# Attention of two layers: scores and products with values as plain fp32 on halves of the array

## The chip, the cores and the metric

The kernel runs on one core of a Trainium2 chip. The metric is the device time of one execution in microseconds, as the median of several runs. The program is one launch that holds four layers of a network.

## The reference

Four layers (kinds A, B, C, A) work on two token streams: 128 context tokens and 512 latent tokens. Layers 0 and 3 are of kind A: attention with 16 query heads of 64 channels over 4 key heads, so 4 query heads share one key head. Latent queries see 256 cached tokens and a window of 128 tokens to either side; context queries see the 128 context tokens. Each head has a sink, a constant score that takes part in the softmax and has no value.

```python
def attend_block(q, k, v, valid, sink):
    scale = q.shape[-1] ** -0.5
    s = jnp.einsum('bqkgd,bskd->bkgqs', q, k, preferred_element_type=jnp.float32) * scale
    if valid is not None:
        s = jnp.where(valid, s, -jnp.inf)
    if sink is not None:
        sk = jnp.broadcast_to(sink.astype(jnp.float32)[None, :, :, None, None], s.shape[:-1] + (1,))
        probs = jax.nn.softmax(jnp.concatenate([s, sk], axis=-1), axis=-1)[..., :-1]
...
    return jnp.einsum('bkgqs,bskd->bqkgd', probs.astype(v.dtype), v)
```

Ahead of it stand a dense product to queries, keys and values, a norm of each head and a rotary embedding; behind it a dense product back to 1024 channels. Layer 2 (kind C) has heads of 128 channels and no window; layer 1 is a recurrence. Each layer ends with a channel mixer, a convolution between two large dense products, which take most of the time of the program.

## The kernel before

All work is laid out by hand in the class `Kernel`; a scheduler of the framework sets the final order on each engine. TensorE (PE) multiplies, ScalarE (ACT) and VectorE (DVE) evacuate and compute, GpSimd (POOL) takes some elementwise work, and SP issues the transfers.

**Two-part operands.** An fp32 number is kept as two parts of the type fp32r: a rounded one (h) and the rest (l). A dense product is then three fp32r products (`mm3`, lines 294 to 296 of the kernel's listing). Splitting costs a copy on ACT and a subtraction on DVE or POOL (`split`, lines 299 and 303 do the copy and the subtraction wherever `split` and `copy` are called).

**Attention of kind A** is cut into 16 units: for each of the 4 key heads (`kv`) the query tiles 0, 1, 2, and 3 together with 4 (tile 4 is the context). A `Unit` has these steps:

- `qprep` (lines 83 to 91): POOL makes the two parts of the queries of 4 heads, side by side as 128 columns; four transposes on PE (line 88); ACT copies the result (`QT`), whose 128 rows are the 64 of h and the 64 of l.
- `kprep` (lines 951 to 972), once per key head, in steps between other work: the keys in two parts, each part twice side by side, so that the transposed `KT` has both parts on 128 rows; 14 transposes (line 967). The values become `V2`: h and l side by side as 128 columns.
- `score(g)` (lines 112, 113): for each run of keys two fp32r products, queries times keys h and queries times keys l, each with all 128 rows. Together they are the complete product of the parts. The scores of a head have 512 columns for tile 0, 256 + 384 for tiles 1 and 2, and 512 and 128 for the unit of tiles 3 and 4. DVE adds the mask and takes the maximum (line 123), ACT does the exponential (line 126).
- `turn(j)` (line 178): the probabilities of one tile of 128 keys are transposed for the 4 heads, 4 fp32 transposes; then they are split to `PTh` (ACT) and `PTl` (DVE), 512 columns each.
- `pv(j)` (lines 203, 204): two products with `V2`, with 512 columns. The output has the products with values h on partitions 0 to 63 and those with values l on partitions 64 to 127.
- `rows`, `spread` (lines 155, 166): the inverse sums as rows, spread over partitions with a product of 8 or 16 rows.
- `out` (lines 224 to 229): the lower part is copied (`low`), two additions on DVE bring the heads to their partitions, a product with the inverse, then the two parts of the output on POOL.

There are 19 key tiles for each key head, so 76 `turn` and 76 `pv` for each of the two layers, and 64 `score`. `attend` emits them interleaved: a score of the next unit, a turn of the current one, and a `pv` two turns late (`LAG`). PSUM has two double banks for scores (`bankA`) and four single banks for everything else (`bankB`): turns, outputs, transposes and dense products share these. Beside this runs work from the list `todo`; in layer 0 that is the modulation of later stages (`mod_row`, line 437), whose four plain fp32 products of 32 columns sit side by side on column groups of the array. The recurrence of layer 1 has plain fp32 products on two column halves (line 1441).

Of the kernel before, what the change touches and what calls it, by code (L numbers as in the profile page):

```python
# [40 lines left out]
class Unit:  # L41
    """Attention of the query heads of one key head, for one or two tiles of 128 queries, in steps."""

    def __init__(self, K, at, kv, ts):
# [29 lines left out]
    def qprep(self):  # L74
        nc, K, dh, G, kv = self.nc, self.K, self.dh, self.G, self.kv
        nb = 1 if self.A else 2      # 128-column blocks of a head's transposed q
        self.QT = []
        for t in self.ts:
            self.at.nq += 1
            o = 1024 + 512 * (self.at.nq % 2)  # L80
            Q2 = self.at.scr[:, o:o + 512].rearrange("p (g d) -> p g d", g=G)
            x = self.at.q[kv][:, t].rearrange("p (g d) -> p g d", d=dh)
# [12 lines left out]
    def score(self, g):  # L95
# [9 lines left out]
        for i, t in enumerate(self.ts):  # L105
            QT = self.QT[i]
            for c0, w, o0 in self.runs[i]:
                out = ps[:, o0:o0 + w]
                kh, kl = KT[:, 0, c0:c0 + w], KT[:, 1, c0:c0 + w]
                if self.A:  # L110
                    qt = QT[:, g * 128:(g + 1) * 128]
                    mm(out=out, lhsT=qt, rhs=kh, start=True, stop=False)  # L112
                    mm(out=out, lhsT=qt, rhs=kl, start=False, stop=True)
                else:
                    K.mm3(out, QT[:, g * 256:g * 256 + 128], QT[:, g * 256 + 128:g * 256 + 256], kh, kl, True, True)
# [16 lines left out]
    def inverse(self):  # L132
        """One over the sums, to which the sink adds its part (A)."""
# [11 lines left out]
        # its two parts, side by side  # L145
# [5 lines left out]
    def rows(self):  # L151
        """The inverses as rows."""
# [1597 lines left out]
```

## Time and profile before

| what | value |
|---|---|
| median of 3 runs | 3316.09 us (3314.82 to 3317.6) |
| span of the profiled execution | 3308.3 us |
| PE / weight loads busy | 94% / 89% of the span |
| DVE / ACT / POOL busy | 66% / 45% / 19% of the span |

The profile is of one execution; its span runs from its first to its last instruction, and no other time of that execution is given. A matmul's record is longer than the time it keeps the engine, because the next one streams in before the last has drained. The distance between the starts of two records tells what one takes. "PEld" is the load of weights ahead of a matmul.

### The profile page before, as it was taken

What the parts mean: (1) busy time and instruction counts of PE and PEld (TensorE: products, weight loads), DVE (VectorE), ACT (ScalarE), POOL (GpSimd) and SP (SyncE); (2) the same over time, 40 slices, a digit from 0 to 9 for tenths busy, and PEclk for the clock granted to TensorE, in tenths of its full rate; (3) what the DMA queues carried; (4) which work ended last, traced back from release to release, by engine and by line L of the source; (5) the groups of instructions that cost most, each with busy time, mean ns of one, the idle gap of its engine ahead of it and who ended that gap; (6) DMA issues with size and microseconds to landing.
All of it is one profiled execution on the core that took longest, in us unless ns stands there. A gap on an engine that the chain in (4) does not pass through costs nothing.

```text
span 3308.3 us, 54925 instructions
## 1 busy us (share of the span) xinstructions
PE 3124.8 (94%) x22108; PEld 2946.5 (89%) x22108; DVE 2198.9 (66%) x4190; ACT 1480.8 (45%) x2524; POOL 640.2 (19%) x1111
## 2 busy tenths in 40 slices
PE   7999999999983899999999999999999999999999
PEld 6867879989872899999999889999999878999999
DVE  6788886776568348666666756777656796645543
ACT  4477442343343525334443664343343585533432
POOL 1432463453333000000002630000001441000000
PEclk8999999999996899999999999999999999999999
DMA  6251555455642423343323012344324202122221
GB/s 242 94 178 46 143 172 156 130 159 147 209 181 98 141 71 115 117 125 97 117 92 103 27 56 73 111 126 123 114 96 141 78 27 83 56 87 76 66 82 52
DMA packets 384798, 364.26 MB, mean 110 GB/s; under 512 B 39656, under 2 KB 358000, under 8 KB 374944
## 3 DMA queue, kind: packets, MB, share of 16 engines
q1 hardware_dynamic: 383264, 356.56, 34.5%
q0 software_dynamic: 1280, 4.20, 0.4%
q8 instruction: 174, 2.85, 0.4%
q14 instruction: 80, 0.66, 0.1%
HBM read 328.07 MB, written 36.83 MB: 110 GB/s over the span
## 4 chain that ended last, share of the span: by engine, by line
PE 76%; DVE 11%; ACT 6%; DMA 3%; POOL 2%; issue 2%; SPq 0%; DVEq 0%; ACTq 0%; POOLq 0%
PE psa L294 16%; PE psa L296 16%; PE psa L295 16%; PE psb L294 6%; PE psb L296 6%; PE psb L295 6%; PE psb L178 2%; DVE wl L303 1%; PE psb L437 1%; ACT wh L299 1%; PE psb L203 1%; DVE Pt L1467 1%; PE psb L204 1%; ACT PTh L299 1%; PE psa L112 1%
## 5 line engine op out<-in xcount | busy, mean ns | idle before, releaser
L294 PE MATMUL psa<-yh,wh 128*128 128x384 f32 (+1 forms) x2752 | 855.0, 311 | 0.9 <-POOL yh L228 0.7
L295 PE MATMUL psa<-yl,wh 128*128 128x384 f32 (+1 forms) x2752 | 851.6, 309 | 1.0 <-POOL yl L229 1.0
L296 PE MATMUL psa<-yh,wl 128*128 128x384 f32 (+1 forms) x2752 | 851.2, 309 | 0.0
L303 DVE TENSOR_TENSOR wl<-raw,wh 128x2048 fp32r<-128x2048 f32 (+2 forms) x192 | 403.5, 2102 | 316.8 <-ACT wh L299 313.1
L299 ACT ACTIVATE wh<-raw 128x2048 fp32r<-128x2048 f32 (+2 forms) x192 | 332.9, 1734 | 490.3 <-PE psa L295 442.5
L294 PEld LDWEIGHTS psa<-yh,wh 128*128 128x128 f32 x2752 | 523.0, 190 | 15.3 <-issue 6.8
L295 PEld LDWEIGHTS psa<-yl,wh 128*128 128x128 f32 x2752 | 523.2, 190 | 2.0 <-POOL yl L229 1.8
L296 PEld LDWEIGHTS psa<-yh,wl 128*128 128x128 f32 x2752 | 522.8, 190 | 0.1
L294 PE MATMUL psa<-ah,wh 128*128 128x384 f32 (+1 forms) x1184 | 367.4, 310 | 5.7 <-DVE X L658 5.7
L296 PE MATMUL psa<-ah,wl 128*128 128x384 f32 (+1 forms) x1184 | 366.3, 309 | 0.0
L295 PE MATMUL psa<-al,wh 128*128 128x384 f32 (+1 forms) x1184 | 365.7, 309 | 0.0
L303 POOL TENSOR_TENSOR yl<-scr,yh 128x256 fp32r<-128x256 f32 (+1 forms) x42 | 44.8, 1066 | 1287.9 <-ACT yh L299 1261.8
L658 DVE SCALAR_TENSOR_TENSOR X<-psa,modt,X 128x256 f32<-128x256 f32 x372 | 141.5, 432 | 220.5 <-PE psa L296 220.5
L294 PEld LDWEIGHTS psa<-ah,wh 128*128 128x128 f32 x1184 | 224.3, 189 | 13.5 <-issue 6.4
L294 PE MATMUL psb<-wh,yh 128*128 128x256 f32 x800 | 228.1, 287 | 1.3 <-ACT yh L597 1.2
L296 PE MATMUL psb<-wh,yl 128*128 128x256 f32 x800 | 226.4, 286 | 2.0 <-POOL yl L303 1.4
L295 PE MATMUL psb<-wl,yh 128*128 128x256 f32 x800 | 226.8, 285 | 1.0 <-DVE wl L303 1.0
L295 PEld LDWEIGHTS psa<-al,wh 128*128 128x128 f32 x1184 | 224.4, 189 | 0.0
L296 PEld LDWEIGHTS psa<-ah,wl 128*128 128x128 f32 x1184 | 224.1, 189 | 0.0
L710 DVE SCALAR_TENSOR_TENSOR t<-hb,cols,t 128x641 f32<-128x641 f32 x176 | 171.7, 977 | 66.3 <-ACT t L708 66.3
L700 ACT ACTIVATE hb<-psa,cols 128x512 f32<-128x512 f32 x320 | 149.9, 519 | 113.4 <-PE psa L296 113.3
L299 ACT ACTIVATE ah<-a 128x640 fp32r<-128x640 f32 x88 | 65.0, 739 | 275.5 <-DVE a L720 275.4
(323 smaller groups left out, 6700.4 us busy)
## 6 DMA issues: line engine op xcount, KB each, us to landing
raw<-in_w_up_dram SPq DMA_DIRECT2D x176, 512.0 KB, 5.1
raw<-in_w_mod_dram SPq DMA_DIRECT2D x51, 1024.0 KB, 4.9
raw<-in_w_mod_dram SPq DMA_DIRECT2D x64, 512.0 KB, 3.8
raw<-in_w_down_dram SPq DMA_DIRECT2D x48, 640.0 KB, 3.9
raw<-in_l_w_qkv_dram SPq DMA_DIRECT2D x20, 1024.0 KB, 6.8
raw<-in_w_down_dram SPq DMA_DIRECT2D x16, 896.0 KB, 4.5
raw<-in_l_w_o_dram SPq DMA_DIRECT2D x12, 1024.0 KB, 5.0
d_w<-s5P SPq DMA_DIRECT2D x64, 128.0 KB, 2.9
```

Of the source, the lines that this page charges most:

```text
L112: mm(out=out, lhsT=qt, rhs=kh, start=True, stop=False)
L178: nc.tensor.transpose(out=pt[:, o:o + 128], in_=self.Ps[g][:, c:c + 128], identity=K.ident)
L203: mm(out=po, lhsT=v, rhs=PTh[:, sl], start=first, stop=False)
L204: mm(out=po, lhsT=v, rhs=PTl[:, sl], start=False, stop=last)
L294: mm(out=out, lhsT=wh, rhs=xh, start=start, stop=False)
L295: mm(out=out, lhsT=wh, rhs=xl, start=False, stop=False)
L296: mm(out=out, lhsT=wl, rhs=xh, start=False, stop=stop)
L299: self.nc.scalar.activation(out=out, in_=in_, func=ACTF.Copy)
L303: (sub or self.nc.vector).tensor_tensor(out=l, in0=x, in1=h.bitcast(F32), op=ALU.subtract)
L658: self.nc.vector.scalar_tensor_tensor(out=self.X[:, d, s0:s1], in0=p[:, o:o + s1 - s0], scalar=m[:, v, gate + d:gate + d + 1], in1=self.X[ ...
L700: nc.scalar.activation(out=hb[:, s0 + o - (s0 // 512) * 512:s1 + o - (s0 // 512) * 512], in_=p[:, b + s0:b + s1], func=ACTF.Identity, bias ...
L710: nc.vector.scalar_tensor_tensor(out=t, in0=hb[:, 0:641], scalar=kc[0], in1=t, op0=ALU.mult, op1=ALU.add)
```

## The change

In layers of kind A all operands stay plain fp32, and the array is used in halves.

- Scores: a head has 64 channels, so queries and keys fill 64 rows. The queries are transposed twice over (on rows 0 to 63 and on 64 to 127). `KT` holds on its first 64 rows the cached keys and the context tile, on its other 64 rows the four latent tiles. Each run of keys is one fp32 product on its half of the rows (`tile_position` (0, 0) or (64, 0)), and the runs of one head on different halves write different banks of PSUM.
- `kprep` makes three copies on ACT, 4 transposes and one copy per key head; there is no `V2`, the raw values are the weights.
- `turn`: one copy to one fp32 tile in place of the split, on DVE for 2 of 5 turns and on ACT for the others. There are twice as many buffers of the one kind of tile.
- `pv`: the four heads by parity. The two even ones (256 columns) go to partitions 0 to 63, the two odd ones to 64 to 127, as two fp32 products with 64 columns of weights on the two halves of the columns.
- `out`: one copy of 256 columns; `low` and the two additions are gone.
- Comments are taken out throughout, which moves line numbers.

```diff
@@ Unit.__init__
             if t == 4:
-                runs, keys, mask = ((768, 128, 512 if self.A else 896),), (6,), 0
+                runs, keys, mask = ((256, 128, 0, 0),) if self.A else ((768, 128, 896),), (6,), 0
             elif self.A and t == 0:
-                runs, keys, mask = ((256, 256, 0), (0, 256, 256)), (2, 3, 0, 1), 384
+                runs, keys, mask = ((0, 256, 256, 1), (0, 256, 512, 0)), (2, 3, 0, 1), 384
             elif self.A and t == 3:
-                runs, keys, mask = ((0, 256, 0), (512, 256, 256)), (0, 1, 4, 5), 0
+                runs, keys, mask = ((0, 256, 256, 0), (256, 256, 512, 1)), (0, 1, 4, 5), 0
             elif self.A:
-                runs, keys, mask = ((0, 256, 256), (128 + 128 * t, 384, 512)), (0, 1, t + 1, t + 2, t + 3), 0
+                runs, keys, mask = ((0, 256, 256, 0), (128 * t - 128, 384, 512, 1)), (0, 1, t + 1, t + 2, t + 3), 0
@@ Unit.qprep
+            if self.A:
+                Q2 = self.at.scr[:, 512 + 512 * (self.at.nq % 2):1024 + 512 * (self.at.nq % 2)]
+                nc.gpsimd.tensor_copy(out=Q2.rearrange("p (g u d) -> p g u d", g=G, u=2),
+                                      in_=x.unsqueeze(2).to_broadcast([128, G, 2, dh]))
+                pq = K.bankB()
+                for g in range(G):
+                    nc.tensor.transpose(out=pq[:, g * 128:(g + 1) * 128], in_=Q2[:, g * 128:(g + 1) * 128],
+                                        identity=K.ident)
+                QT = self.at.sp.tile([128, 512], F32, tag="QT", name="QT", bufs=3)
+                K.copy(QT, pq)
+                self.QT.append(QT)
+                continue
@@ Unit.score
-                    qt = QT[:, g * 128:(g + 1) * 128]
-                    mm(out=out, lhsT=qt, rhs=kh, start=True, stop=False)
-                    mm(out=out, lhsT=qt, rhs=kl, start=False, stop=True)
+                    us = slice(64 * u[0], 64 * u[0] + 64)
+                    mm(out=out, lhsT=QT[us, g * 128:(g + 1) * 128], rhs=KT[us, c0:c0 + w], start=True, stop=True,
+                       tile_position=(64 * u[0], 0))
@@ Unit.turn
+        if self.A:
+            PT = self.PT[j] = self.at.sp.tile([128, 512], F32, tag="PTh", name="PT", bufs=2 * self.at.npt)
+            (nc.vector.tensor_copy if self.at.nt % 5 in (1, 3) else K.copy)(PT, pt)
+            self.at.nt += 1
+            return
@@ Unit.pv
+        if self.A:
+            a, PT = js[0], self.PT.pop(j).rearrange("p (hp par c) -> p par hp c", par=2, c=128)
+            for par in range(2):
+                mm(out=po[64 * par:64 * par + 64, 0:256], lhsT=self.at.vraw[:, self.keys[i][a], self.kv * 64:self.kv * 64 + 64],
+                   rhs=PT[:, par], start=a == 0, stop=a == len(self.keys[i]) - 1, tile_position=(0, 64 * par))
+            if a == len(self.keys[i]) - 1:
+                self.out(i)
+            return
...
-            if self.A:
-                mm(out=po, lhsT=v, rhs=PTh[:, sl], start=first, stop=False)
-                mm(out=po, lhsT=v, rhs=PTl[:, sl], start=False, stop=last)
@@ Unit.out
-        if self.A:
-            low = sp.tile([64, 512], F32, tag="low", name="low", bufs=1)
-            K.copy(low, po[64:128, :])
-            for par in range(2):
-                pv = po[0:64, :].rearrange("p (hp par c) -> p par hp c", par=2, c=128)[:, par]
-                lv = low.rearrange("p (hp par c) -> p par hp c", par=2, c=128)[:, par]
-                nc.vector.tensor_tensor(out=o[64 * par:64 * par + 64], in0=pv, in1=lv, op=ALU.add)
-        else:
-            K.copy(o, po.rearrange("p (h c) -> p h c", h=2))
+        K.copy(o, po[:, 0:256].rearrange("p (h c) -> p h c", h=2))
@@ Kernel.attention, kprep
+            if A:
+                KT = at.KTs[kv] = self.wtile("wh", F32, "KT")[:, 0:512]
+                ks = slice(kv * 64, kv * 64 + 64)
+                self.copy(KA[:, 0:2, 0], kraw[:, 0:2, ks])
+                self.copy(KA[:, 2:4, 0], kraw[:, 6, ks].unsqueeze(1).to_broadcast([128, 2, 64]))
+                self.copy(KA[:, :, 1], kraw[:, 2:6, ks])
+                yield
+                p = self.bankB()
+                for t in range(4):
+                    nc.tensor.transpose(out=p[:, t * 128:(t + 1) * 128], in_=KA[:, t].rearrange("p u d -> p (u d)"),
+                                        identity=self.ident)
+                yield
+                self.copy(KT, p)
+                return
```

The order of PE in layer 3, before, amid the units of the fourth key head (L178 are the transposes of the probabilities, L203 and L204 the products with values, L112 and L113 the scores, L155 and L166 the inverse sums):

```order
L178 MATMUL psb<-ident,PB 128x128 x4
L203 MATMUL psb<-PTh,V_27085 128x512
L112 MATMUL psa<-KT,QT 128x256
L113 MATMUL psa<-KT,QT 128x256
L112 MATMUL psa<-KT,QT 128x384
L155 MATMUL psb<-identR,inv 8x128
L113 MATMUL psa<-KT,QT 128x384
L204 MATMUL psb<-PTl,V_27085 128x512
L178 MATMUL psb<-ident,PB 128x128 x4
L166 MATMUL psb<-rT,sel 128x128 x2
```

The order of PE in layer 3 with the change, at a place of the same kind (L192 are now the transposes of the probabilities, L125 the scores, L217 the products with values, L169 and L180 the inverse sums):

```order
L192 MATMUL psb<-ident,PB 128x128 x4
L125 MATMUL psa<-KT,QT 128x256
L169 MATMUL psb<-identR,inv 8x128
L125 MATMUL psa<-KT,QT 128x384
L217 MATMUL psb<-PT,vraw 64x256 x2
L192 MATMUL psb<-ident,PB 128x128 x4
L180 MATMUL psb<-rT,sel 128x128 x2
L125 MATMUL psa<-KT,QT 128x256
L125 MATMUL psa<-KT,QT 128x384
L217 MATMUL psb<-PT,vraw 64x256 x2
```

Before, only L166 in these rows uses a part of the array; now whole-array transposes, scores on row halves and values on column halves follow one another, and a whole-array transpose of the sums can stand between the two halves of a score.

The order of DVE in layer 3 before, at a last unit of a key head (L123 adds the mask and takes the maximum, L303 makes the low part of a turn, L224 and L227 are the output):

```order
L224 TENSOR_TENSOR o<-psb,low 64x256 x2
L303 TENSOR_TENSOR PTl<-psb,PTh 128x512
L227 TENSOR_TENSOR o<-o,psb 128x256
L123 ISA PB,st<-psa,mask,sink 128x128
L123 ISA st 128x1
L303 TENSOR_TENSOR PTl<-psb,PTh 128x512
L123 ISA PB,st<-psa,mask,sink 128x512
```

The order of DVE in layer 3 with the change (L137 adds the mask and takes the maximum, L196 copies a turn, L153 to L158 are the inverse sums, L240 the output):

```order
L196 COPY PT<-psb 128x512
L137 ISA PB,st<-psa,mask,sink 128x640
L137 ISA st 128x1
L153 TENSOR_TENSOR st<-st,sink 128x4
L157 TENSOR_TENSOR st<-st 128x4
L158 RECIPROCAL st<-st 128x4
L196 COPY PT<-psb 128x512
L137 ISA PB,st<-psa,mask,sink 128x512
```

Before, every turn has its operation on DVE and every output three; now 30 of the 76 turns have one, and an output one.

## Rows read from the trace of the kernel before

**Rows 1.** Windows; columns: stretch in us, length, busy us (instructions) by engine, clock:

```profile
core 0: us, PE busy (x) PEld busy (x) DVE busy (x) ACT busy (x) POOL busy (x), PEclk, DMA share, GB/s
146.60:317.00 170.40, 160.05 (x1043) 116.81 (x1042) 141.43 (x364) 131.10 (x311) 53.43 (x115) 1.00 0.33 113
2621.80:2775.10 153.30, 142.34 (x913) 114.30 (x909) 137.09 (x359) 127.55 (x306) 52.15 (x126) 0.99 0.09 29
```

**Rows 2.** Timeline of PE, layer 3: start, length, engine, line, operands, count:

```profile
2700.18 0.39 PE L203 MATMUL psb<-PTh,V 128*128 128x512 f32 x1
2700.41 0.60 PE L178 MATMUL psb<-ident,PB 128*128 128x128 f32 x4
2700.76 0.30 PE L155 MATMUL psb<-identR,inv 128*8 128x128 f32 x1
2700.90 0.45 PE L204 MATMUL psb<-PTl,V 128*128 128x512 f32 x1
...
2702.57 0.28 PE L112 MATMUL psa<-KT,QT 128*128 128x256 f32 x1
...
2702.80 0.34 PE L112 MATMUL psa<-KT,QT 128*128 128x384 f32 x1
2702.98 0.33 PE L113 MATMUL psa<-KT,QT 128*128 128x384 f32 x1
```

**Rows 3.** Lines of PE in layer 3's stretch: count, busy us, mean ns, idle before:

```profile
L178 PE MATMUL psb<-ident,PB 128*128 128x128 f32 x296 | 48.3, 279 | 3.8 <-ACT QT L299 1.9 <-DVE o L224 1.6 <-ACT rT L299 0.2
...
L112 PE MATMUL psa<-KT,QT 128*128 128x256 f32 x85 | 25.5, 311 | 1.1 <-DVE st L123 0.9
```

**Rows 4.** Timeline of PE, layer 0: where parts of the array are used:

```profile
156.21 1.06 PE L437 MATMUL psb<-raw,cond 128*32 128x512 f32 x8
157.21 0.45 PE L967 MATMUL psb<-identR,scrR 128*128 128x128 f32 x3
157.49 0.47 PE L203 MATMUL psb<-PTh,V 128*128 128x512 f32 x1
157.80 0.40 PE L204 MATMUL psb<-PTl,V 128*128 128x512 f32 x1
158.12 0.62 PE L437 MATMUL psb<-raw,cond 128*32 128x512 f32 x1
...
219.97 0.60 PE L178 MATMUL psb<-ident,PB 128*128 128x128 f32 x4
220.49 0.43 PE L166 MATMUL psb<-rT,sel 8*128 8x128 f32 x2
220.86 0.55 PE L178 MATMUL psb<-ident,PB 128*128 128x128 f32 x3
```

**Rows 5.** Timeline of PE ahead of layer 1: a transpose with 64 rows:

```profile
339.63 0.27 PE L1174 MATMUL psb<-ident,four 64*128 64x64 f32 x1
339.83 0.41 PE L1214 MATMUL psb<-ident,raw 128*64 128x128 f32 x2
```

**Rows 6.** Timeline of PE in layer 1: plain fp32 on two column halves:

```profile
965.15 5.06 PE L1441 MATMUL psb<-yh,raw 128*64 128x80 f32 x140
```

**Rows 7.** Lines of DVE in layer 3's stretch:

```profile
L303 DVE TENSOR_TENSOR PTl<-psb,PTh 128x512 fp32r<-128x512 f32 x75 | 51.3, 686 | 7.4 <-ACT PTh L299 6.2
...
L224 DVE TENSOR_TENSOR o<-psb,low 64x256 f32<-64x256 f32 x36 | 14.9, 415 | 2.7 <-ACT low L299 1.6 <-POOL inv L149 0.6
```

**Rows 8.** Lines of ACT in layer 3's stretch:

```profile
L299 ACT ACTIVATE PTh<-psb 128x512 fp32r<-128x512 f32 x74 | 43.8, 595 | 21.1 <-PE psb L178 18.4 <-PE psb L155 1.8 <-PE psa L113 0.2
```

**Rows 9.** Lines of DVE at the start: a plain copy from PSUM:

```profile
L412 DVE COPY X<-psb 128x512 f32<-128x512 f32 x10 | 6.4, 685 | 3.6 <-PE psb L410 3.6
```

**Rows 10.** Timeline of PE ahead of layer 0's stretch:

```profile
122.25 0.54 PE L967 MATMUL psb<-identR,scrR 128*128 128x128 f32 x4 [2.35 <-DVE cols L377]
123.90 0.58 PE L112 MATMUL psa<-KT,QT 128*128 128x256 f32 x1 [1.11 <-ACT KT L299]
```

**Rows 11.** Windows, the columns of rows 1:

```profile
123.40:130.20 6.80, 6.30 (x33) 6.30 (x33) 5.49 (x15) 4.71 (x9) 1.14 (x2) 0.50 0.01 2
```

More of the change, by code (lines that the diff above doesn't have):

```diff
@@ L79, in qprep @@
             self.at.nq += 1
+            x = self.at.q[kv][:, t].rearrange("p (g d) -> p g d", d=dh)
+            if self.A:
[10 more added lines that the diff above has]
+                continue
             o = 1024 + 512 * (self.at.nq % 2)
             Q2 = self.at.scr[:, o:o + 512].rearrange("p (g d) -> p g d", g=G)
[L82 removed]
             nc.gpsimd.tensor_scalar(out=Q2[:, :, 0:dh], in0=x, scalar1=1.0, scalar2=0.0, op0=ALU.mult, op1=ALU.add)
@@ L106, in score @@
             QT = self.QT[i]
-            for c0, w, o0 in self.runs[i]:
+            for c0, w, o0, *u in self.runs[i]:
                 out = ps[:, o0:o0 + w]
-                kh, kl = KT[:, 0, c0:c0 + w], KT[:, 1, c0:c0 + w]
                 if self.A:
-                    qt = QT[:, g * 128:(g + 1) * 128]
-                    mm(out=out, lhsT=qt, rhs=kh, start=True, stop=False)
-                    mm(out=out, lhsT=qt, rhs=kl, start=False, stop=True)
+                    us = slice(64 * u[0], 64 * u[0] + 64)
+                    mm(out=out, lhsT=QT[us, g * 128:(g + 1) * 128], rhs=KT[us, c0:c0 + w], start=True, stop=True,
+                       tile_position=(64 * u[0], 0))
                 else:
+                    kh, kl = KT[:, 0, c0:c0 + w], KT[:, 1, c0:c0 + w]
                     K.mm3(out, QT[:, g * 256:g * 256 + 128], QT[:, g * 256 + 128:g * 256 + 256], kh, kl, True, True)
@@ L191, in pv @@
         if i not in self.po:
-            if self.A or i == 0:
-                self.po[i] = K.bankB()[:, 0:N]
-            else:
-                self.po[i] = K.bankB()[:, 0:N]
+            self.po[i] = K.bankB()[:, 0:N]
         po = self.po[i]
+        if self.A:
[6 more added lines that the diff above has]
+            return
         PTh, PTl = self.PT.pop(j)
@@ L201, in pv @@
             v = self.at.V2s[self.kv][:, self.keys[i][a]]
-            if self.A:
-                mm(out=po, lhsT=v, rhs=PTh[:, sl], start=first, stop=False)
-                mm(out=po, lhsT=v, rhs=PTl[:, sl], start=False, stop=last)
-            else:
-                K.mm3(po, v[:, 0:dh], v[:, dh:2 * dh], PTh[:, sl], PTl[:, sl], first, last)
+            K.mm3(po, v[:, 0:dh], v[:, dh:2 * dh], PTh[:, sl], PTl[:, sl], first, last)
         if a == len(self.keys[i]) - 1:
@@ L855, in attention @@
         kraw = qp.tile([128, 7, kvc], F32, name="kraw")
-        vraw = qp.tile([128, 7, kvc], F32, name="vraw")
+        vraw = at.vraw = qp.tile([128, 7, kvc], F32, name="vraw")
         nc.sync.dma_start(out=kraw[:, 0:2], in_=i["cache_l%d_k" % l][0].rearrange("(t p) h d -> p t (h d)", p=128))
@@ L946, in attention @@
         at.KTs, at.V2s = {}, {}
-        scr = at.scr = self.nrm.tile([128, 2944], R, tag="scr", name="scrR")
-        at.nq = 0
-        K2 = scr[:, 0:1024].rearrange("p (t s d) -> p t s d", t=4, s=2)
-        def kprep(kv):
+        at.nq = at.nt = 0
+        scr = at.scr = self.nrm.tile([128, 2944], F32 if A else R, tag="scr", name="scrR")
+        if A:
+            KA = scr[:, 0:512].rearrange("p (t u d) -> p t u d", t=4, u=2)
+        else:
+            K2 = scr[:, 0:1024].rearrange("p (t s d) -> p t s d", t=4, s=2)
+        def kprep(kv):
+            if A:
+                KT = at.KTs[kv] = self.wtile("wh", F32, "KT")[:, 0:512]
[11 more added lines that the diff above has]
+                return
             KT = at.KTs[kv] = self.wtile("wh", name="KT")[:, 0:1792].rearrange("p (s n) -> p s n", s=2)
@@ L956, in kprep @@
                 src = kraw[:, t0:t1, kv * dh:(kv + 1) * dh]
-                if A:
-                    kb = src.unsqueeze(2).to_broadcast([128, n, 2, 64])
-                    self.split(K2[:, 0:n, 0].rearrange("p t (u d) -> p t u d", u=2),
-                               K2[:, 0:n, 1].rearrange("p t (u d) -> p t u d", u=2), kb)
-                else:
-                    self.split(K2[:, 0:n, 0], K2[:, 0:n, 1], src)
+                self.split(K2[:, 0:n, 0], K2[:, 0:n, 1], src)
                 yield
```

1 line of the change is left out of this document (removed).

## The prediction

> **What bounds the kernel now.** The table of windows comes first, for the two stretches in which this attention runs: from the first to the last product with the values, 170.4 us in layer 0 and 153.3 us in layer 3 [rows 1]. No engine is full there. PE shows 142 of 153 us, but its records overlap, so that share says little; DVE stands at 137.1 and ACT at 127.6. TensorE's clock is granted in full (1.00 and 0.99), so the rows used below are rows at 2.4 GHz.
>
> PE's own need I take from the distance between starts in the timeline. A 512-column product with the values takes 0.23 us (2700.18 to 2700.41). Four fp32 transposes take 0.35 to the next start, and that next, small one stands 0.14 where 0.06 would do, so 0.109 each. Two score products of 256 columns take 0.23, one of 384 takes 0.18; a narrower one goes in proportion, 0.06 with 128 [rows 2]. A part-wise transpose of Q or K takes 0.09 (three in the 0.28 from 157.21) [rows 4]. With the counts of layer 3 (the rows give them for the two largest groups [rows 3], PE's order for the others): 296 transposes x 0.109 = 32.3; 152 products with values x 0.231 = 35.1; scores 170 x 0.117 + 58 x 0.174 + 32 x 0.058 = 31.9; 106 transposes of Q and K x 0.09 = 9.5; the small rest, spreading of the inverses included, about 10. Together **119 us** in a stretch of 153.
>
> **Going from the whole array to a part of it costs time too**, and the trace has it in several places [rows 4]. Four transposes begin at 219.97, the two 8-row products of L166 at 220.49, whole-array transposes again at 220.86. The trip takes 0.89; its work at the usual pace is 4 x 0.109 + 2 x 0.058 = 0.55. So 0.34 us for two switches, **0.17 each**. Within it the engine empties first, about 0.09: a 512-column product ahead of L437 keeps the engine for 0.32 (157.80 to 158.12) in place of 0.23. Then the first weight load lies open. With 32-column weights that load is short: L437's four products take 1.00 where two passes of 512 columns need 0.85, so 0.15 on leaving and 0.09 on entering, 0.24 for two switches or 0.12 each. A 64-row product behaves alike: 0.20 between starts at L1174, where 0.06 to 0.11 would do [rows 5].
>
> Along PE's order before there are 66 such switches in the stretch of layer 0 and 34 in that of layer 3. At 0.17 layer 3 needs 119 + 6 = 125 us, and PE waits for the other 28. Layer 0 has 16 groups of L437's four products, 0.86 each, 12 us more than layer 3's few: 131 + 11 = 142, again 28 of waiting. A chain fills that time: ACT stood idle 18.4 us for PE's transposes [rows 8], DVE 6.2 us for ACT's copy [rows 7], and only after DVE's subtraction is the bank of a turn free again for PE.
>
> **The products themselves come out even.** A plain fp32 product is two passes. The two column halves of L1441 run together: 140 records with 80 columns, 70 pairs, in 5.06 us, 0.072 a pair [rows 6], 0.90 ns a column and pass. L437's row gives 0.83 (0.85 us over 1024 columns) [rows 4]. I take 0.85, so 0.435 for 256 columns.
> - Values: 76 key tiles x 0.435 = 33.1 in place of 35.1.
> - Scores: the longer half sets the time. 12 heads of the first tile of queries 0.435; 30 of the second and third 0.65 (384 against 256 columns); 16 of the last unit 0.435 + 0.22, as its context tile follows on a half already used. 5.2 + 19.5 + 10.5 = 35.2 in place of 31.9.
> - Transposes of Q go to 0.109, those of K from 38 to 8 in the stretch: 76 x 0.109 = 8.3 in place of 9.5.
>
> So 119 us again, nothing either way.
>
> **The switches don't.** Along the new PE order there are 271 in layer 0 and 255 in layer 3: scores, whole-array transposes and values alternate. That is 205 and 221 more. No row has a 64-row or 64-column product of this length amid transposes, so the price is bounded by the two round trips: 0.12 and 0.17. I take 0.17, since 128-column weights (scores) and the whole-array work that follows are the kind of L166's trip, and only the 64-column weights of the values lie between. 221 x 0.17 = 37.6 and 205 x 0.17 = 34.9. PE then needs 119.3 + 43.4 = 162.7 in layer 3 and 131.1 + 46.1 = 177.2 in layer 0, both **over the whole present stretch**.
>
> **DVE and ACT get lighter, on a path that no longer decides.** DVE in layer 3 loses 75 subtractions of 686 ns (51.4) and 36 sums of 415 (14.9) [rows 7], and gains 30 copies of 685 ns, 20.5 [rows 9]: from 137 to about 91, less with K's parts gone. ACT makes 46 in place of 76 copies of 595 ns [rows 8]: from 128 to about 110, less with a narrower copy of the output. The bank of a turn is free after one copy in place of two operations in a row. So PE's 28 us of waiting should mostly go; the bounds are 0 and 28, and I take 5, as both engines fall below 70% of the new stretch. POOL's two operations per tile of Q become one of twice the width, and it loses the parts of V: it stands idle for most of the stretch (52 of 153 us busy) [rows 1], so that counts nothing. No transfer is touched.
>
> **Ahead of the stretch** of layer 0, PE idles 2.35 and 1.11 us in the preparation of the first keys [rows 10], and the clock stands at 1.2 GHz (0.50) for the 6.8 us from 123.4, when the engine works again [rows 11]; that costs about 3.4 more. With 4 transposes for 14 and no wait for a second part, 1 to 7 us can go. The wait for the bank of the columns stays behind DVE's queue, so I take 3.
>
> **The sum.** Layer 3: 162.7 + 5 - 153.3 = +14.4. Layer 0: 177.2 + 5 - 170.4 = +11.8. Less 3: **+23 us**. The profiled execution has a span of 3308.3 us; the runs' median, 3316.09, is 7.8 more, which I take as what lies around a span. 3316.1 + 23 = **3339 us**. With 0.15 and 0.20 a switch and 2 to 10 us of waits a layer this case reaches from 3323 to 3365.
>
> **Rivals.**
> - *Faster: only the emptying counts.* If the weights of the new halves are loaded while the engine empties, a switch costs 0.09. For it: weights load ahead everywhere inside one mode. Against it: both round trips show more. 119.3 + 23.0 + 5 = 147.3 and 131.1 + 24.4 + 5 = 160.5, less 3: -19, 3297 us. It decides below about 0.11 a switch.
> - *Even: the lower row.* At 0.12: 154.9 and 168.6, less 3: -3, 3313 us; without any wait 3303.
> - *The halves of the rows don't run together*, so that the change doesn't do what it says. No row of this trace has two row groups at work at once; the column groups that do (L437, L1441) share all rows. One after the other, 64 heads a layer pay 0.435 more each: +56 over the forecast, 3395 us. The Trainium skill ("TensorE: Matmul & The Clock Gate", Part 3: Packing small matmuls) has tiles in different row groups start some 4 ns apart, and a pack of four reach 3.07 times one tile's rate; by that rule the forecast's pair stands, and no run here shows it yet.
> - *The waits stay.* If the copies remain behind other work in their queues and PE still waits 28 us a layer: 190.7 and 205.2, less 3: +69, 3385 us. The lighter engines speak against it.
> - *The weights of the second pass lie open.* L1441's 0.072 a pair leaves next to nothing beside the stream [rows 6], so there they don't. If they did with the values: L166's pair takes 0.37, of which 0.12 is the stream and 0.09 the emptying, so two open loads of 128 columns cost 0.16, one of 64 about 0.04; 76 x 2 x 0.04 x 2 layers = +12 over the forecast, 3351 us. The same section of the Trainium skill lets a weight load overlap a running product only where the row group differs, which it does not between column halves; the trace disagrees, with those 0.072 us.
>
> **How the numbers follow.** The forecast's case has 0.52, only-the-emptying 0.14, the even case 0.13, serial halves 0.12, staying waits 0.05, open second loads 0.04. Slower takes the forecast and the three dear rivals: 0.73; within 0.2% (6.6 us, about what a measurement of this kernel can tell) the even case: 0.13; faster 0.14. The range runs from 3297, the centre of the cheap case, to 3375: the forecast, the even case, the open loads and half of the cheap case, leaving out serial halves, staying waits and the lower half of the cheap case.
>
> **What would show it.** Right: some 0.435 us from a pair's start to the end of its second pass, with 0.15 to 0.2 extra at each change of mode; both stretches longer by 10 to 15 us; DVE under 91 and ACT under 110 us in them; few idle gaps of PE that name a copy. Wrong: the second row half starting 0.4 us after the first (serial halves); next to nothing extra at a change of mode, with stretches under 150 and 165 us; or PE idle ahead of the values for copies that are queued behind exponentials. Outside the two stretches nothing but the start of layer 0 should differ.

## The result, and the profile after

The changed kernel takes **3335.16 us** (median of 4 runs, 3326.3 to 3339.91), the kernel before 3316.85 in the same comparison: ratio **1.0052**, 95% interval 1.0039 to 1.0065. It is slower by 0.5% (18.3 us, where the forecast had 23), which is the forecast's side, and 4 us below its number (3339).

The table of windows of the changed kernel, over the two stretches from the first to the last product with values; the columns are those of [rows 1]:

```profile
core 0: us, PE busy (x) PEld busy (x) DVE busy (x) ACT busy (x) POOL busy (x), PEclk, DMA share, GB/s
142.10:323.10 181.00, 179.91 (x1152) 91.80 (x1150) 100.13 (x271) 107.57 (x275) 41.85 (x97) 1.00 0.32 107
2640.50:2803.70 163.20, 163.20 (x1035) 88.89 (x1033) 97.83 (x269) 106.33 (x276) 42.17 (x97) 1.00 0.11 34
```

Against [rows 1] the stretches went from 170.4 to 181.0 and from 153.3 to 163.2 us. PE now fills layer 3's stretch to the last hundredth, and DVE and ACT, at 137 and 128 us before, are down to 98 and 106. The clock is granted in full in both, so this is no matter of the clock. What PE does with the time is in its timeline of layer 3 (start, length, line, operands, count; L125 scores, L217 values, L192 turns):

```profile
2704.86 0.65 PE L217 MATMUL psb<-PT,vraw 128*64 128x256 f32 x4
2705.44 0.66 PE L192 MATMUL psb<-ident,PB 128*128 128x128 f32 x4
2706.03 0.92 PE L125 MATMUL psa<-KT,QT 64*128 64x256 f32 x6
2706.88 0.65 PE L217 MATMUL psb<-PT,vraw 128*64 128x256 f32 x4
2707.46 0.66 PE L192 MATMUL psb<-ident,PB 128*128 128x128 f32 x4
2708.05 0.92 PE L125 MATMUL psa<-KT,QT 64*128 64x256 f32 x6
2708.89 0.65 PE L217 MATMUL psb<-PT,vraw 128*64 128x256 f32 x4
```

Read the distances between starts: a key tile of values takes 0.58 us (2704.86 to 2705.44), a turn 0.59, a score of six records 0.85 (2706.03 to 2706.88). Nothing idles between them, and between the same neighbours they come out alike all through the layer, to 0.01 us. In [rows 2] the four transposes of a turn went at 0.109 each, 0.436 together; here, between two partial modes, the same four take 0.585. (A mode is the way the array is used: whole, or as tiles of fewer rows or columns.) The work did not grow; each block pays for its way in and out.

DVE and ACT have changed sides. Their lines in layer 3's stretch, with the idle time before them and who ended it; first DVE's mask in the kernel before, then DVE and ACT with the change:

```profile
L123 DVE CUSTOM_DVE_ANT_0 PB<-psa,mask,sink 128x512 f32<-128x512 f32 (+1 forms) x74 | 51.6, 710 | 2.0 <-PE psa L113 1.4
```

```profile
L137 DVE CUSTOM_DVE_ANT_0 PB<-psa,mask,sink 128x640 f32<-128x640 f32 (+2 forms) x75 | 52.6, 718 | 31.0 <-PE psa L125 30.3 <-POOL inv L162 0.3
L196 DVE COPY PT<-psb 128x512 f32<-128x512 f32 x30 | 20.7, 689 | 8.6 <-PE psb L192 8.1
```

```profile
L312 ACT ACTIVATE PT<-psb 128x512 f32<-128x512 f32 x45 | 26.6, 591 | 21.1 <-PE psb L192 20.2 <-PE psb L169 0.7
```

DVE stood idle 30.3 us for scores of PE, where the line of its mask had 1.4 before; its copies cost what [rows 9] promised (689 against 685 ns). PE was the waiting engine, now the others wait for PE.

### The profile page after: what moved, and what is told of

Read it like the earlier page. It is cut to its first block, busy times and chain, and to the rows that moved or that the text cites. A ratio compares the mean times of both kernels' runs of the same rounds, so it can differ in the third digit from the quotient of the medians.

```text
span 3336.7 us, 55009 instructions
## 1 busy us (share of the span) xinstructions
PE 3169.9 (95%) x22332; PEld 2897.7 (87%) x22332; DVE 2108.5 (63%) x3986; ACT 1430.5 (43%) x2456; POOL 607.3 (18%) x1063
## 4 chain that ended last, share of the span: by engine, by line
PE 79%; DVE 10%; DMA 4%; ACT 3%; POOL 2%; issue 2%; SPq 0%; DVEq 0%; POOLq 0%; ACTq 0%
PE psa L307 16%; PE psa L309 16%; PE psa L308 16%; PE psb L307 6%; PE psb L309 6%; PE psb L308 6%; PE psb L192 3%; PE psa L125 3%; PE psb L217 3%; DVE wl L316 1%; PE psb L450 1%; ACT wh L312 1%; DVE Pt L1494 1%; DVE scr L598 1%; DVE t L725 1%
```

## The experiments

"Stretch" is from the start of the first to the end of the last product with values of a layer in the profiled execution (0.2 to 0.7 us more than the windows above, which end near the last one's start), "start" what lies ahead of layer 0's, "between" what lies between the two. "Switches" are changes between the whole array, row halves, column halves and the small row and column tiles, counted along PE's order; the transposes of the inverse sums, with 8 or 16 columns, are counted as whole-array work. A run exceeds its span by 1.8 us (3338.46 against 3336.7). Behind layer 3's stretch all have 532.5 to 533.1.

| kernel | switches, layers 0 / 3 | start | stretch, layer 0 | between | stretch, layer 3 | ratio to before |
|---|---|---|---|---|---|---|
| before | 66 / 34 | 146.7 | 171.0 | 2304.2 | 153.9 | |
| the change | 271 / 255 | 142.2 | 181.3 | 2317.2 | 163.4 | 1.0052 (1.0039 to 1.0065) |
| e1: values in halves alone | 211 / 195 | 144.9 | 169.8 | 2319.1 | 153.3 | 1.0019 (1.0010 to 1.0029) |
| e2: scores in halves alone | 208 / 194 | 141.1 | 188.2 | 2312.1 | 168.9 | 1.0093 (1.0078 to 1.0108) |
| e3: change, wide spread | 248 / 229 | 143.1 | 178.0 | 2317.5 | 159.9 | 1.0039 (1.0027 to 1.0051) |
| e4: before, wide spread | 36 / 2 | 146.1 | 169.8 | 2310.1 | 153.5 | 0.9988 (0.9979 to 0.9997) |
| e5: change, in twos | 214 / 180 | 145.1 | 181.3 | 2309.8 | 161.9 | 1.0069 (1.0054 to 1.0084) |
| e6: e1, in twos | 158 / 134 | 147.7 | 165.9 | 2317.5 | 146.7 | 0.9997 (0.9988 to 1.0006) |
| e7: change, parts of V kept | 271 / 256 | 142.2 | 184.4 | 2309.2 | 164.0 | 1.0066 (1.0054 to 1.0079) |
| e8: e6, wide spread | 140 / 114 | 150.4 | 163.8 | 2320.2 | 144.8 | 0.9984 (0.9975 to 0.9993) |
| e9: before again | 66 / 34 | 146.5 | 171.1 | 2305.5 | 154.4 | 1.0001 (0.9991 to 1.0011) |
| e10: change again | 271 / 255 | 141.9 | 181.3 | 2305.5 | 163.4 | 1.0040 (1.0025 to 1.0055) |
| e11: e8, scores singly | 138 / 114 | 146.4 | 166.7 | 2317.5 | 147.9 | 0.9982 (0.9973 to 0.9991) |

### The two halves of the change apart

e1 takes `turn`, `pv` and `out` from the change and keeps two-part scores:

```diff
@@ Unit.pv, against the kernel before
+                mm(out=po[64 * par:64 * par + 64, 0:256], lhsT=self.at.vraw[:, self.keys[i][a], self.kv * 64:self.kv * 64 + 64],
+                   rhs=PT[:, par], start=a == 0, stop=a == len(self.keys[i]) - 1, tile_position=(0, 64 * par))
```

> Values on column halves alone: one copy per turn, raw values as weights, the short output; queries, keys and scores stay in two parts. Along PE's order the switches are 211 in layer 0's stretch and 195 in layer 3's (271 and 255 with the whole change, 66 and 34 before). Switch theory (PE pays its products plus about 0.17 us a switch, 0.15 for those into 64-column weights): PE needs 117 + 195 x 0.15 = 146 us in layer 3 and 129 + 211 x 0.15 = 161 in layer 0, with DVE and ACT relieved, so stretches of 148 to 153 and 163 to 170 (before 153.3 and 170.4, the change 163.2 and 181.0); the run 0 to 15 us faster than before. Rival, the plain fp32 halves themselves are dear and the switches cheap: the values carry as much of the loss as the scores, stretches near 158 and 176, slower than before by about 10. Rival, DVE and ACT decide in any case: 135 to 140 in layer 3.

Measured: stretches of 169.8 and 153.3 us, as before to 1.2 us, with PE busy 152.66 of 153.40 in layer 3. The idle gaps of PE (11.0 us in that stretch before) are gone, taken up by the switches and by halves that run alone: 16 of 83 blocks of values in layer 3 have only half a key tile and take 0.58 us all the same. The whole kernel is 0.2% slower, where 0 to 15 us faster was expected; its stretches do not explain that (below).

e2 takes `qprep`, `kprep` and `score` from the change and keeps two-part values, with `V2` made on POOL:

```diff
@@ Unit.pv, against the changed kernel
-                mm(out=po[64 * par:64 * par + 64, 0:256], lhsT=self.at.vraw[:, self.keys[i][a], self.kv * 64:self.kv * 64 + 64],
-                   rhs=PT[:, par], start=a == 0, stop=a == len(self.keys[i]) - 1, tile_position=(0, 64 * par))
...
+                mm(out=po, lhsT=v, rhs=PTh[:, sl], start=first, stop=False)
+                mm(out=po, lhsT=v, rhs=PTl[:, sl], start=False, stop=last)
```

> Scores on row halves alone: plain fp32 queries and keys; turns split in two parts, values with two-part operands, output with its additions as before. Switches 208 and 194. Switch theory: PE needs 121 + 194 x 0.17 = 154 us in layer 3 and 133 + 208 x 0.17 = 168 in layer 0, and DVE stays near 130 with the split behind it, so waits stay as well: 160 to 172 and 175 to 188, as slow as the whole change or slower, though it has 60 switches a layer fewer. Rival, the halves are dear: the same sign, so this run alone does not tell; together with the values alone it must give more than the sum of both losses. Rival, DVE and ACT decide: near the 153.3 and 170.4 of before.

Measured: 188.2 and 168.9 us, dearer than both halves together. The losses of the two parts against the kernel before, -1.2 and -0.6 us for e1 and +17.2 and +15.0 here, add up to more than the whole change loses (+10.3 and +9.5); with dear halves the whole would have to lose more than that sum. PE's timeline in layer 3 shows why this part alone is so dear:

```profile
2708.03 0.70 PE L125 MATMUL psa<-KT,QT 64*128 64x256 f32 x2
2708.66 0.66 PE L192 MATMUL psb<-ident,PB 128*128 128x128 f32 x4
2709.24 0.70 PE L125 MATMUL psa<-KT,QT 64*128 64x256 f32 x4
2709.87 0.50 PE L214 MATMUL psb<-PTh,V 128*128 128x512 f32 x1
2710.21 0.40 PE L215 MATMUL psb<-PTl,V 128*128 128x512 f32 x1
2710.53 0.70 PE L125 MATMUL psa<-KT,QT 64*128 64x256 f32 x2
```

A block of two records of 64 x 256 takes 0.63 us (2708.03 to 2708.66), and so does a block of four (2709.24 to 2709.87): the four are two halves side by side, the two are one half that runs alone. Here 39 of 81 blocks of scores have two records, in the changed kernel 9 of 63, and the scores take 59.5 us from start to start in place of 49.4. So row halves gain only as long as the order of PE keeps the two runs of a head together, and when they meet a whole-array product between them they pay twice. The halves themselves do run together: in the changed kernel's trace the records of a pair start 5 to 8 ns apart, mostly 6 or 7. The Trainium skill ("TensorE: Matmul & The Clock Gate", Part 3: Packing small matmuls) has tiles of different row groups start some 4 ns apart; the trace agrees to a few nanoseconds.

### The price of a switch

e3 is the change with the spread product brought from 8 or 16 rows to all 128, zeros below, so that its block is no longer a mode of its own; e4 is the same edit in the kernel before:

```diff
-        self.rT = rT[0:m]
+        self.rT = rT
...
-                                 lhsT=self.at.sel[0:2 * n * self.G, i, b], rhs=self.rT, start=True, stop=True)
+                                 lhsT=self.at.sel[:, i, b], rhs=self.rT, start=True, stop=True)
...
-        at.sel = qp.tile([16, 2, 2, 128], R, name="sel")
...
+        at.sel = qp.tile([128, 2, 2, 128], R, name="sel")
...
+        at.rTs = [qp.tile([128, 128], R, name="rTs%d" % n) for n in range(2)]
```

> The change, but the product that spreads the inverses has 128 rows (zeros below) in place of 8 or 16, so that it uses the whole array; nothing else differs. Its products take as long as before; the switches fall from 271 to 248 and from 255 to 229. Switch theory with PE as the only bound: 23 x 0.17 = 4 us less in layer 0 and 26 x 0.17 = 4.4 less in layer 3, so stretches of 177 and 159 and a run 8 us faster than the change. Rival, a switch costs next to nothing beside the dear halves, or passes while PE waits: no difference (within 1 us a stretch).

Measured: 3.3 us less for 23 switches and 3.5 for 26, **0.14 us a switch**. One place in the timelines shows a single trip. First the changed kernel, then e3:

```profile
2659.22 0.66 PE L192 MATMUL psb<-ident,PB 128*128 128x128 f32 x4
2659.81 0.43 PE L180 MATMUL psb<-rT,sel 8*128 8x128 f32 x2
2660.17 0.55 PE L192 MATMUL psb<-ident,PB 128*128 128x128 f32 x3
2660.65 0.65 PE L217 MATMUL psb<-PT,vraw 128*64 128x256 f32 x2
```

```profile
2657.22 0.66 PE L193 MATMUL psb<-ident,PB 128*128 128x128 f32 x4
2657.64 0.42 PE L181 MATMUL psb<-rTs,sel 128*128 128x128 f32 x2
2657.89 0.51 PE L193 MATMUL psb<-ident,PB 128*128 128x128 f32 x3
2658.33 0.65 PE L218 MATMUL psb<-PT,vraw 128*64 128x256 f32 x2
```

From the first start to that of the second transposes: 0.95 us with two switches, 0.67 without, 0.14 each. Up to the next block of values, which takes in what the second transposes still lose, it is 1.43 against 1.11, so 0.16 each. The columns that stream are the same, only the rows differ.

> The kernel before, with only the spread product brought to 128 rows (zeros below), so that its stretches have 36 and 2 switches of mode in place of 66 and 34. By my account PE is not the bound of the kernel before: 4.2 to 4.5 us less need of PE (30 and 32 switches at the 0.14 us that the same edit gave in the changed kernel) should change the stretches (171.0 and 153.9 us, first to last product with values) by less than 2 us each. If PE's own path set the end there too, they lose 4 each. It is also the control for the time between the two stretches, 2304.2 us in the profile of the kernel before and 2310 to 2319 in all five kernels with an edit so far: if any shift of the start of what follows brings that growth, this one has 2310 to 2319 too and the total is 3318 to 3325; if only the removal of parts from the attention brings it, it has 2303 to 2306 and the total is 3309 to 3315.

Measured: 1.2 and 0.4 us less for 30 and 32 switches. The same edit that gave 3.5 us where PE is the bound gives next to nothing where it is not. That is the plainest sign that the bound moved: in the kernel before a switch was hidden under a wait. The other half of the expectation came out mixed: 2310.1 us between the stretches in the profile, as one case had it, and a total of 3310.63 us, as the other had it. As a whole this kernel is 0.12% faster than the one before (0.9988), more than its stretches lose.

e5 emits turns, values and scores of the changed kernel in twos:

```diff
+                    for _ in range(min(PAIR, len(S)) if at.A else 1):
...
+                k = min(PAIR, len(T)) if at.A else -(-len(T) // (len(S) + 1))
...
+                    while len(late) >= 2 * PAIR:
+                        after(len(late) - PAIR)
```

> The change with the same instructions in another order: turns, values and scores are emitted in twos, so PE's order has 214 and 180 switches in place of 271 and 255. Switch theory: 57 x 0.17 = 9.7 us less in layer 0 and 75 x 0.17 = 12.8 less in layer 3 if PE stays the bound: stretches of 171 and 151, the run some 22 us faster than the change and near before or a little under it. Rival, the halves are dear: the order changes nothing, 181 and 163. Rival, waits: with scores in twos PE waits for DVE's maxima and for banks, and the stretches fall by less than half of that, with idle gaps of PE that name DVE or ACT.

Measured: nothing in layer 0, 1.5 us in layer 3. Its timeline of PE in layer 3 has both halves of the story:

```profile
2698.03 1.08 PE L218 MATMUL psb<-PT,vraw 128*64 128x256 f32 x8
2699.05 1.57 PE L126 MATMUL psa<-KT,QT 64*128 64x256 f32 x12
2700.55 0.66 PE L90 MATMUL psb<-ident,scrR 128*128 128x128 f32 x4
2701.05 1.04 PE L193 MATMUL psb<-ident,PB 128*128 128x128 f32 x8
2701.84 0.30 PE L170 MATMUL psb<-identR,inv 128*8 128x128 f32 x1
2702.70 1.08 PE L218 MATMUL psb<-PT,vraw 128*64 128x256 f32 x8 [0.56 <-ACT QT L313]
```

Two key tiles of values behind each other take 1.02 us (2698.03 to 2699.05), one alone took 0.58: 0.43 is the work and **0.15** the way in and out. Two heads of six score records take 1.50, one took 0.85: 0.65 and **0.20**. The grouping does what it should. But PE waits at 2702.70, and ACT's timeline tells for what:

```profile
2700.97 0.72 ACT L141 ACTIVATE PB<-PB,st 128x512 f32<-128x512 f32 x1 [1.36 <-DVE st L138]
2701.59 0.19 ACT L141 ACTIVATION_READ_ACCUMULATOR PB<-PB,st 128x1 f32 x1
2701.69 0.39 ACT L141 ACTIVATE PB<-PB,st 128x128 f32<-128x128 f32 x1
2701.98 0.19 ACT L141 ACTIVATION_READ_ACCUMULATOR PB<-PB,st 128x1 f32 x1
2702.07 0.57 ACT L313 ACTIVATE QT<-psb 128x512 f32<-128x512 f32 x1
```

The copy of Q's transposes, which PE had issued by 2701.05, stands behind two exponentials. Of the 161.9 us PE is idle 6.9 in gaps.

Layer 0 is another matter: PE is idle there for only 2.7 us, 1.6 more than without the grouping. Its timeline shows what took the gain (L451 is the line of the modulation's four products of 32 columns, L437 in the kernel before):

```profile
181.59 1.04 PE L451 MATMUL psb<-raw,cond 128*32 128x512 f32 x2
182.57 1.08 PE L218 MATMUL psb<-PT,vraw 128*64 128x256 f32 x8
183.58 1.06 PE L451 MATMUL psb<-raw,cond 128*32 128x512 f32 x6
184.57 1.13 PE L126 MATMUL psa<-KT,QT 64*128 64x256 f32 x8
```

The scheduler has torn a group apart: one of the four products alone takes 0.98 us (181.59 to 182.57), the other three 0.99, and eight records together take 1.00 elsewhere. In layer 0 these products stand in 22 blocks that take 22.0 us from start to start, in place of 18 and 17.9, and 20 of the 53 blocks of values hold a half alone, in place of 8 of 79. With 0.215 us of work for each further half (half of 0.43), that is about 4.1 + 2.6 us, and 1.6 of idle time, where 57 switches at 0.15 were to give 8.6; this is an estimate from those counts. Doubling the grain of the work took switches out, put waits in and tore halves apart, and the sum hardly moved.

### The grouping where waits are rarer

e6 is e1 in twos by e5's edit, e8 is e6 with e3's edit, e11 is e8 with scores one at a time:

```diff
-                    for _ in range(min(PAIR, len(S)) if at.A else 1):
+                    for _ in range(1):
...
```

> The kernel with values on column halves and scores as before (210 and 195 switches along PE's order), with turns, values and scores emitted in twos: 158 and 134 switches. By 0.148 us a switch, as the blocks of four value products show (0.583 us a key tile alone, 1.014 for two behind each other), PE's need falls by 7.8 and 9.0 us; PE was busy through the stretches of 169.8 and 153.3 us. If the copies keep up, the stretches are 162 and 144.5; if PE then waits for copies and exponentials, as it did when the changed kernel was grouped so (6.9 us of gaps in layer 3 and almost nothing gained), they stay within 2 us of 169.8 and 153.3.

> Values on column halves, scores as before, everything in twos and the spread product on 128 rows: 140 and 114 switches. Against the same without the wide spread, 18 and 20 switches less at 0.14 us: 2.5 and 2.8 us less in the stretches where PE is the bound, nothing where it waits for copies. If neither copies nor exponentials hold it, the stretches are 159.5 and 141.7 and the kernel is ahead of the one before by about 15 us unless the time between the stretches takes it back; if they hold it, it stands within 0.3% of the one before.

> Values on column halves, scores on the whole array as before, the spread product on 128 rows, turns and values in twos, but scores one at a time: 138 and 114 switches, as many as with scores in twos too (163.8 and 144.8 us). So what it changes is waits alone. In that kernel the scores of layer 3 take 42.0 us from start to start, where their work is 31.9 by the rows of the kernel before: up to 10 us in which PE stands at a score for a bank that an exponential's input still holds. If grouping the scores brought these waits, the stretches lose 2 to 6 us each and the kernel is 0.25 to 0.5% ahead of the one before; if they come from the turns' copies, the stretches stay within 1.5 us.

Measured: e6 gains 3.9 and 6.6 us on e1 where 7.8 and 9.0 were to be had, so half to three quarters; e8 2.1 and 1.9 more where 2.5 and 2.8 were. What is missing in e6 is torn halves again. From e8's layer 3, whose blocks of values are the same as e6's:

```profile
2696.06 0.65 PE L207 MATMUL psb<-PT,vraw 128*64 128x256 f32 x2
2696.64 0.44 PE L180 MATMUL psb<-ident,PB 128*128 128x128 f32 x2
2697.00 1.08 PE L207 MATMUL psb<-PT,vraw 128*64 128x256 f32 x6
2698.01 0.38 PE L113 MATMUL psa<-KT,QT 128*128 128x256 f32 x1
```

Two key tiles are eight records, 1.02 us side by side; here two of them take 0.58 and the other six 1.01. Blocks that hold a half alone are 30 and 28 in e6, 14 and 16 in e1. Each costs 0.215 us of work more, so 3.4 and 2.6 us for those that came in addition, by this estimate nearly all of the 3.9 and 2.4 that are missing. PE is idle in gaps for 2.3 and 2.7 us in e6, 2.6 and 3.1 in e8.

The stretches of e8 are 7.2 and 9.1 us shorter than before, and with 3309.09 us (3302.82 to 3314.71, 11 runs) against 3315.31 it is ahead of **both** kernels, by 0.16% with an interval of 0.07 to 0.25%. That gain is not shown to be the grouping's: e4, the kernel before with the wide spread alone, has 3310.63 us in the same comparison, and e6, without the wide spread, stands level with the kernel before (0.9997). e11 fell on the other side of its expectation: with as many switches its stretches are 2.9 and 3.1 us longer than e8's, so the grouping of scores helped and did not bring the waits. In the whole it stands where e8 does (0.9982).

### What lies between the stretches

The profile of the change has 13 us more between the stretches than that of before, where nothing was changed. e7 tests one cause: without `V2` one buffer in the ring of the weights comes round earlier. It makes `V2` on POOL, unused:

```diff
                 self.copy(KT, p)
+                yield
+                V2 = at.V2s[kv] = self.wtile("wl", name="V2")[:, 0:14 * dh].rearrange("p (t n) -> p t n", t=7)
+                self.split(V2[:, :, 0:dh], V2[:, :, dh:2 * dh], vraw[:, :, kv * dh:(kv + 1) * dh], nc.gpsimd)
                 return
```

> The changed kernel, but POOL still makes the two parts of the values for each key head into a buffer of the weights' ring, unused; PE's order has one switch more. It tells whether the missing turn of that ring moves the loads of weights behind the attention and brings the 13 us that the profile of the changed kernel shows between the two stretches (2317.2 in place of 2304.2). If so: 2303 to 2307 us between them, total 3320 to 3327, and runs as close together as those of the kernel before (5 us). If not: 2310 to 2319, total 3328 to 3340. The stretches stay at 181 and 163 us within 1.5 either way.

Measured: 3334.2 us (3333.59 to 3344.13). The total is the second case's; the time between, 2309.2 us in its profile, falls between the two cases, so this run alone does not clear the ring. e10 below does: without `V2` it has less between the stretches than this one. (Layer 0's stretch holds 6.8 us with TensorE's clock granted at half, which makes the 184.4 where 181 was expected.)

e9 and e10 are the two kernels without an edit, for a second profile of each:

> The kernel before, unchanged, for a second profile of it. Its first one has a span of 3308.3 us and 2304.2 us between the stretches, every other kernel has 2309 to 2320 there, and the runs of the kernel before go from 3309.8 to 3319.6 us, where that span and the 1.8 us by which a run here exceeds its span make 3310. If that first profile was a short draw: 2306 to 2313 us between the stretches, the stretches again 171 and 154 within 1 us, and the spread of the time lies between the stretches. If the kernel before is really shorter there than all others: 2302 to 2306 again.

> The changed kernel, unchanged, for a second profile of it: stretches again 181 and 163 us within 1. Between them 2317.2 us the first time, with a run of 3338.5 us where the runs go from 3326 to 3340. If what lies between the stretches is scatter that belongs to no kernel, this value moves with the run's own time: run minus stretches (344.6), start (142.2), end (532.7) and 1.8; a run near the median of 3335 has 2314, one of 3327 has 2306. If the change lengthens it: at least 2314 whatever the run.

Measured: the windows between the stretches of e9, and then of e10:

```profile
317.60:2623.10 2305.50, 2173.73 (x15669) 2081.45 (x15668) 1549.46 (x2840) 958.73 (x1521) 482.76 (x773) 0.97 0.39 120
```

```profile
323.20:2628.70 2305.50, 2172.84 (x15659) 2081.17 (x15659) 1544.34 (x2828) 955.90 (x1518) 477.45 (x766) 0.97 0.39 120
```

The same 2305.5 in both. By its own lines e9 fell into the case of a kernel that is shorter there than all others, and e10 refutes that case. The changed kernel had 2317.2 in its first profile and 2305.5 in its second, as the run's own time of 3326.59 us had it in the expectation, while its stretches stayed at 181.3 and 163.4 to 0.1 us. So the 13 us are no part of the change. With both middles equal the spans are 3310.0 and 3324.8: **+14.8 us**, which is +10.2 in layer 0, +9.0 in layer 3, -4.6 ahead of layer 0 and +0.2 behind. In medians of runs the change costs +18.3 us in the first comparison and +14.0 in e10's. In e10's the middle (median run less 1.8 and the profile's other parts) is 2309.7 against 2310.8 for the kernel before; in the first it is 2313.8 against 2310.8.

TensorE's clock tells most of the difference. In the trace's record of the granted clock it stands at half (1.2 GHz) for 139.9 us between the stretches in the first profile of the change and for 122.9 in the second (116.1 and 122.9 in the two of the kernel before). If PE's work sets the pace there, 17 us more at half cost 8.5 of the 11.7 us; that is an estimate, no run separates it.

For e1 and the kernels made of it this does not close. By the same account of medians e1 has 2318 between the stretches, where the kernel before had 2307 in that comparison; e6 has 2318, e8 and e11 have 2315, against 2309 to 2310 (e2 and e5, with 2312, are 5 above it too). Nor does the clock close it: less half of the time at half clock, the profiles of e1, e6, e8 and e11 have 2251 to 2255 us between the stretches, those of the two kernels 2244 to 2247. Something costs them 4 to 11 us there, over many runs, and no run here tells what.

## Why the prediction was right, and where not

**The work came out even, and its terms hold.** By e5's blocks a key tile of values costs 0.43 us (forecast 0.435), a score of the last unit 0.65 (0.435 + 0.22), and four transposes 0.436. A second load of the values' weights does not lie open: two passes of 256 columns fit the 0.43. The rival of open loads is out, as is that of serial row halves (5 to 8 ns between the two starts).

**The switches decide, at the assumed size.** The forecast took 255 x 0.17 + 119.3 = 162.7 us for layer 3. The stretch takes 163.2 with PE never idle, so 0.172 on average. That so near a match came of one price is in part luck. The mean hides three prices: 0.14 to 0.16 for the small row tile (e3), 0.15 around values and turns, 0.20 around scores; and it holds the work of halves that run alone (6 blocks of values and 9 of scores in layer 3), which the forecast did not have. The forecast took the upper of its two bounds, 0.17, for the 128-column weights of the scores; it is too low for them and too high for the others, and the two even out. The lower bound, 0.12, lies below all three. The Trainium skill ("TensorEngine Tiling (Array Packing)", Key Properties) says that a change of tiling mode drains the engine; the trace agrees so far as a product ahead of a change keeps the engine longer (0.32 us in place of 0.23), and adds that this, 0.09 by the forecast's reading of [rows 4], is only a part of the price. The two cheap rivals, emptying alone and 0.12, fall with these numbers.

**The waits went, further than forecast.** "I take 5" a layer was too much: 1.1 us of gaps in layer 0, none in layer 3. Layer 3 thus came out at 163.2 and not 167.7. In layer 0 two errors met: PE is busy for 179.9 in place of 177.2, and the stretch of 181.0 lies near the 182.2 forecast because the waits were overestimated by 4. That is luck.

**Ahead of layer 0** the gain is 4.5 to 4.6 us, where 3 was taken of 1 to 7. Of the waits of [rows 10], 3.5 us, 1.3 are left (0.7 for the keys, 0.6 for the columns, where the forecast let the wait for the columns stay), and the half clock of [rows 11] is gone; the same 6.8 us of the span in the changed kernel, in the columns of [rows 1]:

```profile
123.40:130.20 6.80, 6.46 (x50) 5.72 (x51) 6.66 (x25) 4.54 (x12) 2.70 (x7) 1.00 0.00 0
```

**Wrong: "less than 91" for DVE in layer 3.** It is 97.8. The records of DVE overlap: those of the stretch add up to 157.9 us before, where the busy time is 137.1 [rows 1]. The step subtracted 51.4 + 14.9 of record time from a busy time. Records went down by 48.8 (157.9 to 109.1), near the 45.8 net that the step had, but busy time only by 39.3. ACT's "under 110" held with 106.3.

**Wrong: "the runs' median is 7.8 more, which I take as what lies around a span".** It is 1.8; the other 6 are then a profiled execution that ran short of the median, as e9's did (3311.79 us, the shortest of its ten runs). And "outside the two stretches nothing but the start of layer 0 should differ" is true of the change (e9, e10) but not of any two profiles: between the stretches the same program differs by 12 us from one execution to another. That 3335 us came so near to 3339 is therefore in part luck: held against the +14.8 of the second profiles, the +23 missed by 5.4 us in layer 3, the waits that did not come, and by 1.6 each in layer 0 and ahead of it.

## What to carry to other kernels

A change that lightens two engines is worth what the third has left: count what the third must do after it, its changes of mode among them, before counting what the others save. Packing the array by halves needs blocks of one mode that are long against 0.15 to 0.2 us, so group them, but no further than the copies keep up; and see in the timeline that the scheduler leaves the halves of a pair beside each other, for a half alone costs as much as both. When a profile differs in a place that the change does not touch, take a second profile of both kernels, and compare the granted clock, before looking for a cause.

## What the runs showed of the hardware

- Going in and out of a partial mode costs 0.14 to 0.20 us a switch beyond the stream, most (0.20) around products with 64 rows and 128 columns of weights, 0.14 to 0.16 around 8 rows, 0.15 around 64 columns.
- A score on one row half alone takes as long as two halves side by side: 0.63 us for two records and for four (e2). So does half a key tile of values on one column half: 0.58 us, as the whole (e8).
- The same program took 2305.5 and 2317.2 us over the same untouched work in two executions, all else equal to 0.3 us; the clock stood at half for 17 us more of the longer one. Runs of the kernel before take 3309.8 to 3321.6 us.
